# A hybrid decoder layer: the time mixing in three groups of eight heads, two heads' small matmuls side by side

## The chip, the core and the metric

The kernel runs on one core of a Trainium2 chip. The core has a matrix engine (TensorE, PE in the profile), a vector engine (VectorE, DVE), a scalar engine (ScalarE, ACT), a general one (GpSimd, POOL) and a queue that issues DMAs (SyncE, SP). Each works through its own instructions in the order in which they were placed, and waits on semaphores for the others. TensorE writes into eight PSUM banks of 128 partitions x 512 fp32. The metric is the device time of one execution in microseconds.

## What is computed

One layer for 256 tokens of width 4096, in fp32. A normed input is projected once; three mixers use the columns: RWKV-7 time mixing (24 heads of 64 channels), forgetting attention (FoX, 24 heads of 64) and cross attention to 256 memory tokens (4 heads of 256). Their gated outputs go through one output projection, are normed and added to the input.

```python
h = rms_norm(x, g_pre)
p = h @ w_in                                    # 4096 x 14616
# time mixing, for each head, over the tokens t:
Sa = einsum('bhij,bhj->bhi', S, a_t)
S = S * w_t + Sa[..., None] * b_t + v_t[..., None] * k_t
y_t = einsum('bhij,bhj->bhi', S, r_t)
# forgetting attention, for each head:
s = q @ k.T * scale + cum[q] - cum[k]           # causal
o = softmax(s) @ v
# all three:
y = concatenate([y_rwkv * silu(g_rwkv), y_fox * silu(g_fox), y_mem * silu(g_mq)])
out = x + rms_norm(y @ w_out, g_post)
```

## The kernel before

Every weight tile of 512 KB is loaded by SP, split into a high part (ACT, line 193) and a low part (DVE, line 194), and multiplied with the split input. A transposed projection (`proj_t`) of 128 channels does 32 steps of one 512-wide matmul (high part with both parts of the input, line 211) and one 256-wide (low part, line 213) into one accumulator bank of the ring `pj`; `join` (lines 219 to 223) then adds the two halves, ACT reading one and DVE the other. A projection with the tokens on the partitions (`proj_n`, lines 240 to 242) uses two banks and three matmuls a step: the memory values, the FoX values (256 columns at a time) and the output projection (512 columns).

The program has three stages: the memory branch (to about 440 us), the two mixers (to about 1700 us) and the output projection. In the mixers the 24 RWKV heads go in six groups of two pairs. A pair is 128 channels: the even head lies on partitions 0 to 63, the odd one on 64 to 127. `rwkv_group` does, for each pair, the projections of key, receptance and value with the token shift, the decays, the products inside the four chunks of 64 tokens (`gp`, line 529: four chunks of one head, then of the other, 64 x 128 fp32 matmuls, each of two passes) and the transposes of the keys (`bt`, line 539). The gate's projections follow. Then comes the chain: the inverse of a triangular matrix for each head and chunk, in 31 steps of a DVE product and a DVE sum over eight blocks at once (lines 571 and 573) and two sets of 32 x 32 matmuls (`zp`, `ep`, lines 587 and 595); and the four chunks in turn, each with the value transposes (`tv`, line 614), the right-hand side (`rp`, line 619), its copy R (line 621), the update (`up`, line 625), two copies, the state product (`sp`, line 632) and the output (`yp`, lines 642 and 644, pair by pair). Norm, bonus and gate end the group. `fox_pair` does one pair of the forgetting attention: three projections, the logits `sf` (lines 750, 751), softmax, transposes, and the value products `of` (lines 779, 780: one head, then the other). The list FOX_AFTER says which pairs follow which group.

What the small matmuls use of the 128 x 128 array stands in the profile as rows*columns: 64*128 for `gp`, `bt`, `tv` and `sf`, 128*64 for `rp`, `sp`, `of` and the first part of `yp`, 64*64 for `up` and the rest of `yp`, 32*32 for the inverse; the projections use 128*128.

The order on each engine is set by a planner before the run: it takes the program's instructions by priority (the order of the program, with the weight loads and splits ahead) as soon as its own estimate of the times says that their inputs and buffers are there. Where an instruction waits, other ready work is placed ahead of it.

PSUM: three banks for `pj`, two `ch` (chain), two `fx` (FoX), one `el` (the rest of the pairs' work).

Of the kernel before, what the change touches and what calls it, by code (L numbers as in the profile page):

```python
# [8 lines left out]
F32 = mybir.dt.float32  # L9
# [21 lines left out]
# column offsets of the parts of w_in  # L31
# [5 lines left out]
# forgetting-attention pairs that follow each group of the time mixing  # L37
FOX_AFTER = ((0, 1), (2, 3), (4,), (5, 6), (7,), (8, 9, 10, 11))


def _tiles_order():
    t = [("mem", 128 * i) for i in range(8)]
    for h in range(4):
        t += [("in", O_MQ + 256 * h + 128 * j) for j in range(2)]
        t += [("in", O_GM + 256 * h + 128 * j) for j in range(2)]
    t += [("in", O_WL), ("in", O_AL)]
    for g in range(6):
        for o in (O_R, O_K, O_V, O_GR):
            t += [("in", o + 256 * g + 128 * j) for j in range(2)]
        for p in FOX_AFTER[g]:  # L50
            t += [("in", o + 128 * p) for o in (O_FQ, O_FK, O_GF)]
    return t
# [4 lines left out]
# order of the channel tiles of w_out's rows, as they are done (rwkv 0 .. 11, fox 12 .. 23, mem 24 .. 31)  # L57
Y_ORDER = list(range(24, 32)) + list(range(0, 10)) + list(range(12, 22)) + [10, 11, 22, 23]
Y_PLACE = {c: i for i, c in enumerate(Y_ORDER)}

# columns of the constants
C_ID, C_MASK, C_CAUS, C_BLK, C_TRI, C_X0, C_ONE, C_SEL, C_END = 0, 128, 256, 384, 512, 640, 896, 1024, 1048


def _constants():
# [9 lines left out]
    dup = (i % 32) // 8  # L75
    x0 = np.zeros((P, 32, 8), np.float32)
    for d in range(4):
        for k in range(8):
            x0[dup == d, d * 8 + k, k] = 1.0
    c[:, C_X0:C_X0 + 256] = x0.reshape(P, 256)  # L80
# [6 lines left out]
# columns of the per-channel parameters (channel = 128 * column + partition)  # L87
# [10 lines left out]
def pack(inputs):  # L98
# [14 lines left out]
    wV = np.empty((6, P, KT, 256), np.float32)  # L113
    for i in range(6):
        wV[i] = w_in[:, O_FV + 256 * i:O_FV + 256 * i + 256].reshape(KT, P, 256).transpose(1, 0, 2)
    wO = np.empty((8, P, KT, 512), np.float32)
    wo = w_out.reshape(KT, P, D)[Y_ORDER]
    for i in range(8):
        wO[i] = wo[:, :, 512 * i:512 * i + 512].transpose(1, 0, 2)
    wL = np.ascontiguousarray(w_in[:, O_FL:O_FL + NH].reshape(KT, P, NH).transpose(1, 0, 2))  # L120
    # adapters: [128, pair, 128 decay | 128 iclr]
# [11 lines left out]
        "cst": _constants(),  # L133
# [7 lines left out]
class Layer:  # L141
    def __init__(self, tc, a, ctx, dbg=None):
# [9 lines left out]
        self.pj = pool(name="pj", bufs=3, space=PSUM)  # L152
        self.bg = pool(name="bg", bufs=1, space=PSUM)

# [1 line left out]
    def slot(self, name):  # L156
        """two channel tiles, both parts: [128, 2, (high, low), 256]"""
        return self.p4.tile([P, 2, 2, T], F32R, tag="p4", name=name)

    def psb(self, name, tag):  # L160
        return self.bg.tile([P, 512], F32, tag=tag, name=name, bufs=2 if tag != "el" else 1)

    def setup(self):
        nc, cp = self.nc, self.cp
        self.cst = cp.tile([P, C_END], F32, name="cst")
# [9 lines left out]
        ps = self.psb("warm", "fx")  # L175
# [3 lines left out]
        self.blk = self.cst[:, C_BLK:C_BLK + P]  # L179
        self.ones = self.cst[:, C_ONE:C_ONE + P]  # L180
# [16 lines left out]
    def proj_t(self, key, xs, name):  # L197
        """psum [128 columns, 2, 256 tokens] of the weight tile against xs: the sum of both is the product."""
# [17 lines left out]
    def join(self, ps, out, scale=1.0):  # L216
        """scale * (sum of the two halves of a transposed projection)"""
# [7 lines left out]
    def proj_n(self, src, xs, name, pre=None, other=False, late=None):  # L225
        """psum pair [128 tokens, columns]."""
# [19 lines left out]
        for j in range(m):  # L246
# [15 lines left out]
    def rstd_of(self, src, pool, name):  # L262
        """1 / rms of the rows of src: [128 tokens, 2] and as a row on all partitions [128, 256]."""
# [14 lines left out]
        ps = self.psb(f"rb{name}", "el")  # L278
# [6 lines left out]
    def put_y(self, c, y, g, pool):  # L285
        """y * g of channel tile c, kept in DRAM for the output projection."""
# [12 lines left out]
    def mem_phase(self):  # L299
        nc, tc, a = self.nc, self.tc, self.a  # L300
        with tc.tile_pool(name="pm", bufs=2) as pm:
# [3 lines left out]
            def split(i, src, g, ds, rb):  # L305
                """channel tiles 4 i .. 4 i + 3 of src, scaled, into their parts"""
# [18 lines left out]
            for i in range(2):  # L325
# [8 lines left out]
            nc.sync.dma_start(self.cst, a["cst"])  # L334
# [20 lines left out]
            for h in range(4):  # L355
# [9 lines left out]
                sp = self.psb(f"ms{h}", "fx")  # L365
# [16 lines left out]
                tp = self.psb(f"mt{h}", "fx")  # L382
# [6 lines left out]
                op = self.psb(f"mo{h}", "fx")  # L389
# [10 lines left out]
    def shift_mix(self, ps, mu, out, pr, name):  # L400
        """token shift of a [128 channels, 256 tokens] projection."""
# [8 lines left out]
    def head_sums(self, x, name, tag, pr):  # L410
        """sums over the channels of each head, on all of the head's channels."""
        nc = self.nc
        ring = {"tag": "e", "bufs": 8} if tag == "el" else {"tag": "f", "bufs": 3}
        h, l = (pr.tile([P, T], F32R, name=f"{u}{name}", **ring) for u in "hl")
# [7 lines left out]
    def mix_phase(self):  # L422
        nc, tc, a = self.nc, self.tc, self.a
        EV, OD = slice(0, HD), slice(HD, P)
        with tc.tile_pool(name="pr", bufs=1) as pr:
            self.pr = pr
            self.blkr = pr.tile([P, P], F32R, name="blkr")
            nc.vector.tensor_copy(self.blkr, self.blk)
# [433 lines left out]
```

## Time and profile before

| | us |
|---|---|
| median of three executions | 2069.39 |
| lowest, highest | 2068.79, 2069.72 |
| span of the profiled execution | 2068.2 |
| PE busy | 2049.2 (99%) |
| DVE busy | 1358.5 (66%) |
| ACT busy | 1056.1 (51%) |
| weight and other loads | 382.20 MB, 185 GB/s on average |

The busy time of PE is the union of its matmuls, each from its start to a modelled end, and they overlap: a 512-wide matmul lasts 0.40 us in the profile while the next starts 0.23 to 0.24 us later. The share tells whether PE has work, not how fast it does it; what a matmul costs is the distance of the starts in the timeline. A fp32 matmul stands as two instructions in the profile.

### The profile page before, as it was taken

The numbers are of one execution on the slowest core, as the hardware profiler recorded it, in microseconds if no ns is written. First come the engines' busy times: TensorE is split into PE (matmuls) and PEld (weight loads), VectorE is DVE, ScalarE is ACT, GpSimd is POOL, SyncE is SP. The second block draws the span as 40 slices with busy tenths as digits, with TensorE's granted clock in tenths as the row PEclk, the third lists the DMA queues.
The fourth block names the chain that finished last, engine by engine and source line by source line (L and its number), as shares of the span: only waits on it lengthen the run. The fifth ranks groups of instructions, "written<-read, shape, count | busy, mean of one in ns | idle before, by whom it ended". The sixth has DMA issues, their size and how long they took to land.

```text
span 2068.2 us, 31727 instructions
## 1 busy us (share of the span) xinstructions
PE 2049.2 (99%) x12352; PEld 1735.4 (84%) x12352; DVE 1358.5 (66%) x2108; ACT 1056.1 (51%) x1529; POOL 116.3 (6%) x220
## 2 busy tenths in 40 slices
PE   9999999999999999999999999999999999999997
PEld 7888888888988898889888888888898887888886
DVE  6565444476866786678868847797795566444445
ACT  7644544455456544645555455545545456444443
POOL 0292000000000000000000000000000001000000
PEclk9999999999999999999999999999999999999999
DMA  9865555555544555455535544554454468666665
GB/s 364 314 220 180 175 180 171 182 188 173 176 162 144 171 179 166 148 172 167 174 133 167 176 155 141 183 171 154 137 186 147 152 211 287 213 199 198 199 198 183
DMA packets 111274, 382.20 MB, mean 185 GB/s; under 512 B 12540, under 2 KB 17812, under 8 KB 111124
## 3 DMA queue, kind: packets, MB, share of 16 engines
q1 hardware_dynamic: 109332, 373.88, 54.4%
q0 software_dynamic: 1792, 6.29, 0.9%
q8 instruction: 97, 1.59, 0.3%
q14 instruction: 53, 0.43, 0.1%
HBM read 372.23 MB, written 7.89 MB: 184 GB/s over the span
## 4 chain that ended last, share of the span: by engine, by line
PE 96%; POOL 1%; DVE 1%; ACT 1%; DMA 1%; issue 0%; SPq 0%; DVEq 0%; ACTq 0%; POOLq 0%
PE pno L241 5%; PE pno L242 5%; PE pno L240 5%; PE pjkr L211 4%; PE pjq6400f L211 4%; PE pjvr L211 4%; PE pjrr L211 4%; PE pjq7936f L211 4%; PE pjgr L211 4%; PE pjgf L211 4%; PE pjmq L211 3%; PE pjgm L211 3%; PE pnfv L240 2%; PE pnfv L242 2%; PE pnfv L241 2%; PE pjkr L213 2%
## 5 line engine op out<-in xcount | busy, mean ns | idle before, releaser
L194 DVE TENSOR_TENSOR wlno<-rawno,whno 128x1024 fp32r<-128x1024 f32 x128 | 156.6, 1225 | 160.8 <-ACT whno L193 160.7
L193 ACT ACTIVATE whno<-rawno 128x1024 fp32r<-128x1024 f32 x128 | 135.4, 1060 | 173.6 <-PE pno L242 158.2
L241 PE MATMUL pno<-wlno,yp 128*128 128x512 f32 x512 | 199.7, 390 | 1.1 <-DVE wlno L194 1.1
L242 PE MATMUL pno<-whno,yp 128*128 128x512 f32 x512 | 199.3, 389 | 0.0
L240 PE MATMUL pno<-whno,yp 128*128 128x512 f32 x512 | 180.5, 390 | 0.6 <-ACT whno L193 0.6
L211 PE MATMUL pjvr<-x,whvr 128*128 128x512 f32 x384 | 139.9, 401 | 0.0
L211 PE MATMUL pjkr<-x,whkr 128*128 128x512 f32 x384 | 139.1, 400 | 0.0
L211 PE MATMUL pjrr<-x,whrr 128*128 128x512 f32 x384 | 138.9, 399 | 0.0
L211 PE MATMUL pjq6400f<-x,whq6400f 128*128 128x512 f32 x384 | 138.6, 400 | 0.0
L211 PE MATMUL pjgf<-x,whgf 128*128 128x512 f32 x384 | 137.6, 399 | 0.0
L211 PE MATMUL pjq7936f<-x,whq7936f 128*128 128x512 f32 x384 | 136.9, 397 | 0.0
L211 PE MATMUL pjgr<-x,whgr 128*128 128x512 f32 x384 | 135.1, 395 | 0.0
L241 PEld LDWEIGHTS pno<-wlno,yp 128*128 128x128 f32 x512 | 96.1, 188 | 22.0 <-DVE wlno L194 2.2
L240 PEld LDWEIGHTS pno<-whno,yp 128*128 128x128 f32 x512 | 96.0, 188 | 21.4 <-ACT whno L193 1.4
L242 PEld LDWEIGHTS pno<-whno,yp 128*128 128x128 f32 x512 | 96.1, 188 | 20.1
L242 PE MATMUL pnfv<-whnfv,x 128*128 128x256 f32 x384 | 109.5, 286 | 0.0
L241 PE MATMUL pnfv<-wlnfv,x 128*128 128x256 f32 x384 | 109.2, 285 | 0.0
L240 PE MATMUL pnfv<-whnfv,x 128*128 128x256 f32 x384 | 109.1, 287 | 0.0
L213 PE MATMUL pjkr<-x,wlkr 128*128 128x256 f32 x372 | 106.2, 285 | 0.0
L213 PE MATMUL pjvr<-x,wlvr 128*128 128x256 f32 x372 | 106.1, 285 | 0.0
L213 PE MATMUL pjrr<-x,wlrr 128*128 128x256 f32 x372 | 105.8, 284 | 0.0
L213 PE MATMUL pjgf<-x,wlgf 128*128 128x256 f32 x372 | 105.5, 284 | 0.0
(422 smaller groups left out, 5461.6 us busy)
## 6 DMA issues: line engine op xcount, KB each, us to landing
rawno<-in_wO SPq DMA_DIRECT2D x128, 512.0 KB, 4.4
rawkr<-in_wT SPq DMA_DIRECT2D x48, 512.0 KB, 3.5
rawrr<-in_wT SPq DMA_DIRECT2D x48, 512.0 KB, 3.5
rawvr<-in_wT SPq DMA_DIRECT2D x48, 512.0 KB, 3.6
rawgr<-in_wT SPq DMA_DIRECT2D x48, 512.0 KB, 3.6
rawnfv<-in_wV SPq DMA_DIRECT2D x48, 512.0 KB, 3.5
rawq6400f<-in_wT SPq DMA_DIRECT2D x48, 512.0 KB, 3.7
rawq7936f<-in_wT SPq DMA_DIRECT2D x48, 512.0 KB, 3.7
```

The source lines that it names most:

```text
L193: nc.scalar.activation(wh, raw, AF.Copy)
L194: nc.vector.tensor_tensor(wl, raw, f32(wh), ALU.subtract)
L211: nc.tensor.matmul(ps, wh[:, k, :], x.rearrange("p u t -> p (u t)"), start=(kt == 0), stop=last)
L213: nc.tensor.matmul(ps[:, 0:T], wl[:, k, :], x[:, 0, :], start=False, stop=False)
L240: nc.tensor.matmul(ps[t], xh, w[0][:, k, :], start=(kt == 0), stop=False)
L241: nc.tensor.matmul(ps[t], xh, w[1][:, k, :], start=False, stop=False)
L242: nc.tensor.matmul(ps[t], xl, w[0][:, k, :], start=False, stop=(kt == KT - 1))
```

## The change

The RWKV heads go in three groups of four pairs, eight heads (GP = 4), and the code of a group is split in parts: `group_tiles`, `rwkv_pair`, `rwkv_chain`, `rwkv_norm`. A FoX group of four pairs follows each; its values are projected 512 columns at a time (`fox_values`), and the gate's projection and the norm of a pair come after the FoX pairs. The products inside the chunks, the transposes and the FoX logits and value products alternate between the two heads of a pair, which write to two PSUM banks (the value products: to two halves of one). The transposes of the values of all chunks stand in the pair's part beside those of the keys. In the chain the matmuls of all eight heads follow one another in each step, the first half of the output behind the right-hand side, the second behind the state product. `after` makes the first matmul of such a run wait for the last of the run's inputs. The inverse does 16 blocks at once; its start matrix comes by a DMA, and the group's tiles have one buffer instead of two. `proj_n` does the weight tile's steps for the first half of the tokens and then for the second. PSUM: two banks `pj`, three `sm`, two `ch`, one `yp`. The rows of `w_out` are packed in the new order.

```diff
-        self.pj = pool(name="pj", bufs=3, space=PSUM)
+        self.pj = pool(name="pj", bufs=2, space=PSUM)
...
-        return self.bg.tile([P, 512], F32, tag=tag, name=name, bufs=2 if tag != "el" else 1)
+        return self.bg.tile([P, 512], F32, tag=tag, name=name, bufs={"sm": 3, "ch": 2, "yp": 1}[tag])
+
+    def after(self, ins, *others):
+
+        for o in others:
+            self.tc.add_manual_dep(ins.ins, o.ins.name, mybir.DependencyInfo(
+                mybir.DependencyClass.Sync, mybir.DependencyReason.DATA), reason="together")
...
-            for k in range(kc):
-                for t in range(2):
+            for t in range(2):
+                for k in range(kc):
                     mul(j, k, t, w)
...
-                for g in range(6):
-                    self.rwkv_group(g, lr, pr)
-                    for kp in FOX_AFTER[g]:
-                        self.fox_pair(kp, pf)
+                for g in range(NG_):
+                    G = self.group_tiles(g, pr)
+                    for p in range(GP):
+                        self.rwkv_pair(g, p, G, lr, pr)
+                    self.rwkv_chain(g, G, pr)
+                    self.fox_values(g, pf)
+                    for i, norms in enumerate(((0, 1), (2,), (3,), ())):
+                        self.fox_pair(GP * g + i, pf)
+                        for p in norms:
+                            self.rwkv_norm(g, p, G, pr)
...
+        sl = (slice(1, 3), slice(0, 2))
+        gp = [self.psb(f"gp{n}{u}", "sm").rearrange("p (c k t) -> p c k t", c=NCH, k=2) for u in range(2)]
+        for c in range(NCH):
+            for u, hf in enumerate(half):
+                m = nc.tensor.matmul(gp[u][:, c], BK[hf, c, sl[u], :], Tt[u][hf, p, c], start=True, stop=True)
+                if c == u == 0:
+                    self.after(m, at)
...
+        tp = [self.psb(f"bt{n}{u}", "sm").rearrange("p (k c j) -> p k c j", k=2, c=NCH) for u in range(2)]
+        for c in range(NCH):
+            for u, hf in enumerate(half):
+                o = CH * (c + u)
+                nc.tensor.transpose(tp[u][:, 1, c], vp[hf, o:o + P], self.ident[hf, hf])
+        for c in range(NCH):
+            for u, hf in enumerate(half):
+                nc.tensor.transpose(tp[u][:, 0, c], BK[hf, c, sl[u], :], self.ident[hf, hf])
+        for u, hf in enumerate(half):
+            of = half[1 - u]
+            nc.scalar.activation(BKn[:, :, p, u, :], tp[u][:, 0], AF.Copy)
+            nc.scalar.activation(SU[of, :, p, u, :], tp[u][of, 1], AF.Copy)
...
+        X = pr.tile([P, 32, U], F32, name=f"X{N}", tag="X")
+        nc.sync.dma_start(X, a["x0"])
...
+        for c in range(NCH):
+            heads = [(p, u, hf) for p in range(GP) for u, hf in enumerate(half)]
+            rp, yp = ps("rp", c), ps("yp", c, "yp")
+            for p, u, hf in heads:
+                m = nc.tensor.matmul(rp[hf, p, :], Tt[u][:, p, c, 0, :], SU[:, c, p, u, :], start=True, stop=True)
+                if ready is not None and p == u == 0:
+                    self.after(m, ready)
+            for p, u, hf in heads:
+                nc.tensor.matmul(yp[hf, p, :], SU[:, c, p, u, :], Tt[u][:, p, c, 1, :], start=(p == 0), stop=False,
+                                 skip_group_check=True)
+            R = RR[:, c % 2]
+            nc.vector.tensor_copy(R, rp)
+            up = ps("up", c)
+            for p, u, hf in heads:
+                nc.tensor.matmul(up[hf, p, :], Et[hf, NCH * p + c, :], R[hf, p, :], start=True, stop=True)
+            nc.vector.tensor_copy(SU[EV, c, :, 0, :], up[EV])
+            ready = nc.scalar.activation(SU[OD, c, :, 1, :], up[OD], AF.Copy)
+            if c < NCH - 1:
+                sp = ps("sp", c)
+                for p, u, hf in heads:
+                    m = nc.tensor.matmul(sp[hf, p, :], BKn[:, c, p, u, :], SU[:, c, p, u, :], start=True, stop=True)
+                    if p == u == 0:
+                        self.after(m, ready)
+            for p, u, hf in heads:
+                m = nc.tensor.matmul(yp[hf, p, :], SU[hf, c, p, u, :], NG[hf, p, c, 1, :], start=False,
+                                     stop=(p == GP - 1), skip_group_check=True)
...
+    def fox_values(self, g, pf):
+
+        self.vn = pf.tile([P, 2, 512], F32, tag="vn", name=f"vn{g}")
+        ps = self.proj_n(self.a["wV"][g], self.xs, f"fv{g}")
+        for t in range(2):
+            self.nc.scalar.activation(self.vn[:, t, :], ps[t], AF.Copy)
...
+        op = self.psb(f"o{n}", "sm")[:, 0:T]
+        for t in range(2):
+            for u, hf in enumerate(half):
+                c = 128 * (kp % GP) + HD * u
+                m = nc.tensor.matmul(op[hf, P * t:T], vn[:, t, c:c + HD], pts[u][:, T * t:T + P * t],
+                                     start=(t == 0), stop=(t == 1))
+                if t == u == 0:
+                    self.after(m, ready)
```

## Rows read from the trace of the kernel before

**Rows 1.** The page: busy time of each engine, its share of the span, instructions
```profile
PE 2049.2 (99%) x12352; PEld 1735.4 (84%) x12352; DVE 1358.5 (66%) x2108; ACT 1056.1 (51%) x1529; POOL 116.3 (6%) x220
```

**Rows 2.** Waits of PE: waiting group, whom for, us in all, times, longest
```profile
PE pjmk L213 <- DVE wlmk L194: 2.4, 3, 0.9
```

**Rows 3.** Busy time, mixers' stretch: PE, PEld, DVE, ACT, POOL, clock, DMA share
```profile
440.00:1700.00 1260.00, 1260.00 (x8463) 1073.22 (x8462) 928.44 (x1603) 660.27 (x995) 21.76 (x115) 1.00 0.50 164
```

**Rows 4.** Timeline of PE around one run: start, length (us), line, tiles, shapes
```profile
465.78 0.28 PE L213 MATMUL pjrr<-x,wlrr 128*128 128x256 f32 x1
465.90 0.40 PE L211 MATMUL pjrr<-x,whrr 128*128 128x512 f32 x1
466.14 0.28 PE L213 MATMUL pjrr<-x,wlrr 128*128 128x256 f32 x1
466.35 1.16 PE L529 MATMUL gpr<-T0r,BKr 64*128 64x128 f32 x8
467.44 0.51 PE L211 MATMUL pjrr<-x,whrr 128*128 128x512 f32 x1
467.78 0.28 PE L213 MATMUL pjrr<-x,wlrr 128*128 128x256 f32 x1
```

**Rows 5.** Timeline of PE, transposes: keys, values of one head, of both
```profile
479.33 0.46 PE L539 MATMUL btr<-cst,BKr 64*128 64x64 f32 x4
...
608.22 0.33 PE L614 MATMUL tvr<-cst,vpr 64*128 64x64 f32 x2
...
628.86 0.34 PE L614 MATMUL tvr<-cst,vpr 64*128 64x64 f32 x4
```

**Rows 6.** Timeline of PE: chunk steps, with the matmul that follows the long run
```profile
603.91 0.45 PE L632 MATMUL spr<-SUr,BKnr 128*64 128x64 f32 x8
...
605.20 0.50 PE L211 MATMUL pjgf<-x,whgf 128*128 128x512 f32 x1
...
622.69 0.33 PE L632 MATMUL spr<-SUr,BKnr 128*64 128x64 f32 x2
...
637.13 0.45 PE L625 MATMUL upr<-Rr,Etr 64*64 64x64 f32 x8
```

**Rows 7.** Timeline of PE: attention logits of a pair, value products of a head
```profile
574.75 0.50 PE L750 MATMUL sf<-q7936f,q6400f 64*128 64x128 f32 x4
575.07 0.61 PE L751 MATMUL sf<-q7936f,q6400f 64*128 64x256 f32 x4
...
635.27 0.65 PE L779 MATMUL of<-ptf,vn 128*64 128x256 f32 x2
635.75 0.38 PE L780 MATMUL of<-ptf,vn 128*64 128x128 f32 x2
```

**Rows 8.** Busy time of one tile's instructions: pnfv (256 wide), pno (512 wide)
```profile
1157.00:1166.00 9.00, 9.00 (x78) 9.00 (x77) 0.00 (x0) 1.00 0.48 157
...
1900.00:1950.00 50.00, 50.00 (x222) 41.43 (x221) 1.38 (x2) 1.35 (x4) 1.00 0.63 201
```

**Rows 9.** Groups of DVE by line: count, busy us, mean ns, idle before
```profile
L571 DVE TENSOR_TENSOR tmr<-NNr,Xr 128x16 f32<-128x16 f32 (+30 forms) x186 | 79.7, 429 | 4.3
...
L573 DVE TENSOR_REDUCE Xr<-tmr 128x8 f32<-128x16 f32 (+30 forms) x186 | 54.1, 291 | 3.9
```

**Rows 10.** Timeline of DVE: the copy ahead of the update
```profile
633.32 0.29 DVE L621 COPY Rr<-rpr 128x128 f32<-128x128 f32 x1
```

**Rows 11.** Timeline: last matmul of a projection (PE), last read of its bank (DVE)
```profile
574.42 0.39 PE L211 MATMUL pjgf<-x,whgf 128*128 128x512 f32 x1
...
579.72 0.42 DVE L221 TENSOR_TENSOR gf<-pjgf,gf 128x256 f32<-128x256 f32 x1
```

**Rows 12.** Timeline: one chain's first inverse step, block product, last output copy
```profile
530.94 2.02 DVE L564 STREAM_TRANSPOSE NNr<-NGr 128x1024 f32<-128x1024 f32 x1
...
578.99 0.69 PE L587 MATMUL zpr<-Enr,NGr 32*32 32x32 f32 x32
...
664.65 0.28 ACT L645 ACTIVATE Yr<-ypr 128x128 f32<-128x128 f32 x1
```

More of the change, by code (lines that the diff above doesn't have):

```diff
@@ L46, in _tiles_order @@
     t += [("in", O_WL), ("in", O_AL)]
-    for g in range(6):
[L48 to L51, printed above, removed]
+    for g in range(NG_):
+        for p in range(GP * g, GP * g + GP):
+            t += [("in", o + 128 * p) for o in (O_K, O_R, O_V)]
+        for p in range(GP * g, GP * g + GP):
+            t += [("in", o + 128 * p) for o in (O_FQ, O_FK, O_GF, O_GR)]
     return t
@@ L84, in _constants, with _x0 @@
     return c
+def _x0():
+    dup = (np.arange(P) % 32) // 16
+    x0 = np.zeros((P, 32, 16), np.float32)
+    for d in range(2):
+        for k in range(16):
+            x0[dup == d, d * 16 + k, k] = 1.0
+    return x0
 _PCOLS = [("g_pre", 32), ("g_mem", 32), ("mu_rwkv", 38), ("w0", 12), ("a0", 12), ("k_k", 12),
@@ L112, in pack @@
         wN[i] = w_mem[:, 1024 + 512 * i:1536 + 512 * i].reshape(KT, P, 512).transpose(1, 0, 2)
-    wV = np.empty((6, P, KT, 256), np.float32)
-    for i in range(6):
-        wV[i] = w_in[:, O_FV + 256 * i:O_FV + 256 * i + 256].reshape(KT, P, 256).transpose(1, 0, 2)
+    wV = np.empty((3, P, KT, 512), np.float32)
+    for i in range(3):
+        wV[i] = w_in[:, O_FV + 512 * i:O_FV + 512 * i + 512].reshape(KT, P, 512).transpose(1, 0, 2)
     wO = np.empty((8, P, KT, 512), np.float32)
@@ L553, in rwkv_group @@
-        for p in range(2):
-            gps = self.proj_t(("in", O_GR + 128 * (2 * g + p)), self.xs, f"g{N}{p}")
-            self.join(gps, gt[:, p, :])
-            nc.scalar.activation(gt[:, p, :], gt[:, p, :], AF.Silu)
+        Tt, NG, PC, BKn, SU = (G[k] for k in ("T", "NG", "PC", "BKn", "SU"))
+        U = GP * NCH
         ng = NG.rearrange("p a c k t -> p (a c) k t")
@@ L582, in rwkv_group @@
                 nc.gpsimd.memset(Et[rows, :, 0:32], 0.0)
[L584 to L585 removed]
+        zp = self.psb(f"zp{N}", "ch").rearrange("p (u c) -> p u c", u=U)
+        for u in range(U):
             for o in (0, 64):
@@ L588, in rwkv_group @@
                                  start=True, stop=True)
-        Z = f("Z", (P, 8, 32))
-        for o in (32, 96):
-            nc.scalar.activation(Z[o:o + 32], zp[o:o + 32], AF.Copy)
-        ep = self.psb(f"ep{N}", "ch")[:, 0:256].rearrange("p (u c) -> p u c", u=8)
-        for u in range(8):
-            for o in (0, 64):
-                nc.tensor.matmul(ep[o:o + 32, u, :], Z[o + 32:o + 64, u, :], Et[o + 32:o + 64, u, 32:64],
-                                 start=True, stop=True)
-        for o in (0, 64):
-            nc.scalar.activation(Et[o:o + 32, :, 32:64], ep[o:o + 32], AF.Copy)
@@ new lines, in rwkv_chain @@
+        for u in range(U):
+            for o in (0, 64):
+                m = nc.tensor.matmul(ep[o:o + 32, u, :], Z[o + 32:o + 64, u, :], Et[o + 32:o + 64, u, 32:64],
+                                     start=True, stop=True)
+                if u == o == 0:
+                    self.after(m, last)
+        nc.scalar.activation(Et[0:32, :, 32:64], ep[0:32], AF.Copy)
+        nc.vector.tensor_copy(Et[64:96, :, 32:64], ep[64:96])
+        G["Y"] = Y = pr.tile([P, GP, T], F32, name=f"Y{N}", tag="NN")
@@ L616, in rwkv_group @@
-            rp = self.psb(f"rp{N}{c}", "ch")[:, 0:P].rearrange("p (a i) -> p a i", a=2)
-            for p in range(2):
-                for u, hf in enumerate(half):
-                    nc.tensor.matmul(rp[hf, p, :], Tt[u][:, p, c, 0, :], SU[:, p, u, 0, :], start=True, stop=True)
-            R = pr.tile([P, 2, HD], F32, name=f"R{N}{c}", tag="R", bufs=2)
-            nc.vector.tensor_copy(R, rp)
-            up = self.psb(f"up{N}{c}", "ch")[:, 0:P].rearrange("p (a i) -> p a i", a=2)
-            for p in range(2):
-                for u, hf in enumerate(half):
-                    nc.tensor.matmul(up[hf, p, :], Et[hf, 4 * p + c, :], R[hf, p, :], start=True, stop=True)
@@ L639, in rwkv_group @@
-            yp = self.psb(f"yp{N}{c}", "ch")[:, 0:P].rearrange("p (a t) -> p a t", a=2)
-            for p in range(2):
-                for u, hf in enumerate(half):
-                    nc.tensor.matmul(yp[hf, p, :], SU[:, p, u, 0, :], Tt[u][:, p, c, 1, :], start=True, stop=False)
-                for u, hf in enumerate(half):
-                    nc.tensor.matmul(yp[hf, p, :], SU[hf, p, u, 1, :], NG[hf, p, c, 1, :], start=False, stop=True)
-            nc.scalar.activation(Y[:, :, CH * c:CH * c + CH], yp, AF.Copy)
```

389 lines of the change are left out of this document (184 added, 205 removed).

## The prediction

> **What bounds the kernel now.** I read the page first: PE is busy 99% of the span, DVE 66%, ACT 51% [rows 1]. A busy PE can still be waiting, so the next view is PE's own waits: the longest group is 2.4 us in all, in the memory branch [rows 2]; no PE wait at all stands against a small matmul. Then the stretch of the two mixers, 440 to 1700 us, where nearly the whole change lies: PE is busy for all of it at a granted clock of 1.00, the 2.4 GHz level, while DVE is at 928 of 1260 us and DMA at half [rows 3]. So the time is what TensorE's queue takes from start to start, and an edit is worth what it takes out of that queue, unless it makes PE wait. "Busy" does not show that cost (matmuls overlap); the starts in the timeline do.
>
> **What a run of small matmuls costs.** In [rows 4] the big projection matmuls start 0.12 us (256 wide) and 0.24 us (512 wide) after one another. The 256-wide one ahead of the eight score products (L529, on 64 rows of the array) keeps the queue 0.21 us instead, and the 512-wide one behind them 0.34 us. From 466.14 to 467.78 is 1.64 us; less 0.12 and 0.24 the run costs 1.28, which is 0.12 more than its row's own length of 1.16. I price every run that way: length plus 0.12. Two lengths separate the work from the fee for going to another tiling of the array and back: four key transposes of one head take 0.46 and two value transposes 0.33, so a transpose is 0.065 us, and 0.46 + 0.12 - 4 x 0.065 = 0.32 us is the fee of a run [rows 5].
>
> **Two heads at once.** Four value transposes, two of each head (rows 0 to 63 and 64 to 127, each head's result in a bank of its own), take 0.34 us where two of one head take 0.33 [rows 5]. The second head is nearly free. The planner did that by chance here; in the score products it does not occur, since one head's four chunks are written ahead of the other's.
>
> **The change, part by part** (cost on PE's queue, before and after).
>
> Score products: 24 runs x 1.28 = 30.7 us. After: 12 runs with both heads interleaved. If the second head is free, each is as long as one head's run: 12 x 1.28 = 15.4, a gain of 15. If it is not, only 12 fees go: 4. I take 15, as [rows 5] is the same use of 64 rows and two banks.
>
> Transposes: keys 24 x (0.46 + 0.12) = 13.9 us. Values, 48 sets of two: 19 stand alone (0.45 each), 16 lie in eight runs of four (0.46 a run) and 13 join another run (some 0.25), together 15.5. After: the values move out of the chunk steps into the pair's stage, each with both heads interleaved. The keys are ready before the values are mixed, so I count two runs a pair, each 0.58: 13.9. Gain 15.5; 9 if the heads don't overlap (24 x 0.26 more), 19 if both sets go as one run. The copies out of PSUM move along (ACT, half as many and twice as long); no DMA goes with them.
>
> Chunk steps, 24 of them: recurrence right-hand side (like L625), update, and the state/output run: 0.57 + 0.57 + 1.48 = 2.62 us [rows 6] (the last from 603.91 to 605.20, plus 0.19 as 1.28 - 1.09 in [rows 4]). 24 x 2.62, less 6 x 0.23 as the last chunk has no state product, is 61.5; in about 24 places a piece breaks off, as the two at 622.69, at 0.33 + 0.12 each: 72. After: 12 steps of eight heads. Eight matmuls in 0.57 - 0.32 make 0.06 us a pair of heads. A step is 16 pairs (right-hand side and the first half of the output) 1.28, 8 pairs (update) 0.80, and 16 pairs with one change of tiling inside 1.43 (0.15: what 1.48 leaves over 12 pairs and 0.32, in three); 3.51, and 2.88 in the last chunk. 3 x (3 x 3.51 + 2.88) = 40, plus 2 for pieces. Gain 30, bounded by 20 (pieces at the same rate as now) and 32.
>
> Inverse: its two block products fall from 12 runs to 6; 6 x 0.32 = 2.
>
> FoX: the logits already run with both heads interleaved in most pairs [rows 7], so 0. The value products: 0.65 at 635.27 with 0.38 from 635.75 is 0.86, with 0.12 0.98 a head; x24 = 23.5, less 2 as 11 stand right behind another run. After, 12 runs for both heads side by side in columns: 12 if the heads overlap, 12 x (2 x 0.98 - 0.32) = 19.7 if not. The 64-wide ones overlap in columns (0.06 a pair above), a 256-wide pair alone is not shown. I take 12: gain 9.5, bound 2.
>
> FoX values: 1152 matmuls of 256 columns become 576 of 512. 78 in 9.28 us (the last one's 0.28 hangs over) is 0.119 each, 222 in 50.4 is 0.227 [rows 8]: 137 against 131, gain 6. The Trainium skill (TensorEngine Tiling, Instruction Overhead) gives each matmul some 60 cycles; at 2.4 GHz the 576 that go would be worth 14 us, an estimate from that page, and the time 8 us less than forecast. The row shows 2 x 0.119 - 0.227 = 0.011 us for each that goes, under half of it, and the row decides.
>
> Runs of the new kernel will also stand behind one another now and then; at today's rate that is 2 more. Sum of gains: 15 + 15.5 + 30 + 2 + 9.5 + 6 + 2 = 80.
>
> **What lies on other engines.** The inverse's 31 steps run for 16 blocks at once in 3 groups: 93 pairs of operations instead of 186, each at most twice as long, so at most today's 79.7 + 54.1 us of DVE [rows 9]. DVE stays below 80% of the shorter stretch. The matrix X comes by a 256 KB DMA on SP, not a POOL copy: SP's queue holds the weight loads, so a wait for X's buffer would stop those; the buffer's last user is the group before, over 100 us earlier, so 0. Gate projections and norms move behind the chain and only change places with other PE work. Two waits are new. First, the explicit one ahead of each run: all of PE's queue stands behind it. Its cover today: the copy of R ends at 633.61 and the update starts at 637.13, 3.5 us later [rows 6, 10]; so 0; if that cover went, 36 runs would each wait out the rest of a copy, a microsecond or two, some 50 us. Second, projection accumulators fall from three to two banks. A wide FoX-values product needs both free. A projection's last read today ends 5.3 us after its last matmul (574.42 + 0.39 to 579.72 + 0.42) [rows 11]; 1.4 us of six matmuls run before the second bank is needed, so at three places PE stands 0 to 4 us: 0 to 12, and I take 6.
>
> Net 80 - 6 = 74. The profiled span is 2068.2 us, the median 1.2 above it: 2068.2 - 74 + 1.2 = 1995 us.
>
> **Rivals.** (1) The change doesn't do all it says: the planner, which places each instruction by its own estimates, breaks the runs up, or two heads overlap less when each product is two passes of fp32. Then the gains are 4, 9, 20 and 2 in the four places: 35 us less, 2030. For it: about 24 broken steps today; against: [rows 5].
> (2) The chain outlasts its cover, since the group's tiles have one buffer now and the next group can't write them. Today a chain takes from 530.94 to 664.65, 134 us [rows 12], 48 of it inverse. With a doubled inverse it is 182. The cover is a values product (192 x 0.227 = 44) and 16 projections of 32 x 0.36 us: 228. If the chunk steps grew by half as well (86 to 129 us), it would be 225, just inside; 20 us beyond in each group would put the time at 2055.
> (3) Slower: the accumulators. With two banks a projection stands still once the join of the one before last takes over 11.5 us; each of the 84 projections in the mixers would have to lose 0.95 us to eat 80, so joins of 12.5 us where the row has 5.3 (during an inverse, when DVE is fullest). The price at 13 us of join: 84 x 1.5 = 126, less 80: 2115. The Trainium skill (TensorEngine Tiling, PSUM Bottleneck) warns of this: tiling quickens TensorE and not the copies out of PSUM, which can become the bottleneck. The row leaves a factor of two.
>
> **How the numbers follow.** Forecast 0.80, (1) 0.10, (2) 0.05, (3) 0.05. The range's low end takes the better bounds: transposes 3.5, pieces 2, no stall at the banks 6, and 8 for wider merging of runs: 1975. The high end is rival (1) with the stall at 12: 2036. Beyond it lie (2), (3) and a tail: 0.15. About 0.2% (4 us) is what a measurement of this kernel tells from no change. Faster: all but (3) and the far end of (2): 0.93; same 0.02; slower 0.05.
>
> **What would show it.** Right: PE still at 99% with no wait on a small matmul; runs of 16 score products of some 1.16 us; 24 transpose runs near 0.46; three runs a chunk step; values products at 0.227. Wrong: score runs near 2 us; PE waits on the accumulators (idle ahead of L240 or L211) or at the runs' first matmuls; a stretch before the second and third group where PE waits on the chain; a clock below 1.00.

## The result and the profile after

The changed kernel takes 2009.03 us (median of four executions, 2008.06 to 2009.81) beside 2069.09 us of the kernel before on the same chip: a ratio of 0.9708, with a 95% interval of 0.9695 to 0.9722. That is 60 us off, where 74 were forecast. The profiled execution has a span of 2008.0 us. Line numbers from here on are those of the changed kernel.

The page's line of busy times (as in [rows 1]):

```profile
PE 1985.8 (99%) x11776; PEld 1677.8 (84%) x11776; DVE 1317.5 (66%) x1856; ACT 1033.6 (51%) x1439; POOL 113.1 (6%) x196
```

The mixers' stretch (columns as in [rows 3]). The window is put 60 us shorter; in the traces it is 1221.0 us from the first receptance, key or value projection of the mixers to the first matmul of the output projection, where it was 1284.3:

```profile
440.00:1640.00 1200.00, 1198.82 (x7909) 1017.67 (x7908) 889.59 (x1356) 640.58 (x910) 18.28 (x97) 1.00 0.57 173
```

PE's waits (as in [rows 2]):

```profile
PE pno L254 <- DVE wlno L207: 2.8, 3, 1.7
PE pjmk L226 <- DVE wlmk L207: 2.5, 3, 0.9
...
PE tf L823 <- DVE Lf L820: 1.0, 4, 0.4
PE pnfv L254 <- DVE wlnfv L207: 0.7, 3, 0.2
...
PE pjmq L224 <- DVE mk L234: 0.4, 1, 0.4
```

So nothing changed in what bounds the kernel: PE has work for the whole stretch at a granted clock of 1.00, DVE is at 890 of 1200 us, and none of the waits listed stands before a matmul on another tiling than 128*128. Most wait for a part of a weight tile (`wl`, the low part, in three of these). New, beside the short ones at the FoX values (`pnfv`), are two: the FoX transposes `tf` wait for DVE's part of the softmax, and in the memory branch a projection, `pjmq`, waits for DVE's last read of an accumulator bank (the join of `mk`, line 234).

The timeline of PE, which answers [rows 4 to 7]:

```profile
468.70 0.28 PE L226 MATMUL pjrr<-x,wlrr 128*128 128x256 f32 x1
468.91 0.37 PE L552 MATMUL gpr<-T0r,BKr 64*128 64x128 f32 x1
468.92 0.37 PE L552 MATMUL gpr<-T1r,BKr 64*128 64x128 f32 x1
469.13 0.27 PE L552 MATMUL gpr<-T0r,BKr 64*128 64x128 f32 x1
...
469.80 0.27 PE L552 MATMUL gpr<-T1r,BKr 64*128 64x128 f32 x1
469.91 0.40 PE L572 MATMUL btr<-cst,vpr 64*128 64x64 f32 x4
470.15 0.41 PE L575 MATMUL btr<-cst,BKr 64*128 64x64 f32 x4
470.49 0.50 PE L224 MATMUL pjrr<-x,whrr 128*128 128x512 f32 x1
...
474.74 0.46 PE L572 MATMUL btr<-cst,vpr 64*128 64x64 f32 x4
475.04 0.41 PE L575 MATMUL btr<-cst,BKr 64*128 64x64 f32 x4
...
524.78 0.33 PE L656 MATMUL ypr<-T0r,SUr 128*64 128x64 f32 x2
525.04 0.38 PE L226 MATMUL pjvr<-x,wlvr 128*128 128x256 f32 x1
...
669.29 0.33 PE L672 MATMUL ypr<-NGr,SUr 64*64 64x64 f32 x2
669.54 0.50 PE L224 MATMUL pjgr<-x,whgr 128*128 128x512 f32 x1
669.98 0.69 PE L668 MATMUL spr<-SUr,BKnr 128*64 128x64 f32 x16
670.59 0.68 PE L672 MATMUL ypr<-NGr,SUr 64*64 64x64 f32 x14
...
680.72 0.68 PE L662 MATMUL upr<-Rr,Etr 64*64 64x64 f32 x16
681.34 0.39 PE L226 MATMUL pjgr<-x,wlgr 128*128 128x256 f32 x1
...
737.94 0.87 PE L831 MATMUL of<-ptf,vn 128*64 128x256 f32 x8
738.74 0.50 PE L224 MATMUL pjgr<-x,whgr 128*128 128x512 f32 x1
```

Three things are to be seen. The score products go as forecast: T0 and T1 start together, sixteen instructions in 1.00 us (468.91 to 469.91), where eight of one head took 1.09 with the change of tiling behind them [rows 4]. The transposes come one head at a time: four and four of the first head directly behind the products (no fee of their own), those of the second head almost 5 us later in a run of their own. And pieces of the output, two instructions each (one matmul), stand by themselves, at 524.78 in the middle of the pairs' stage and at 669.29 just ahead of the run to which they belong.

Where the 60 us come from. I went through PE's matmuls behind the memory branch in the order of their starts and called every stretch on another tiling than 128*128 a run; its price is the time that it puts between the 128*128 matmuls around it, beyond their usual 0.12 and 0.23 us. The kernel before has 199 runs with 511 changes of tiling, 180.2 us in all; the changed one 108 with 243, 118.4 us: 61.8 off. The FoX values fell from 138.2 to 132.6: 5.6 off. Some 7 came back: the mixers start 2.2 later (at 420.3 us, where it was 418.1), the output projection has 1.7, gate and value projections 2 to 3, the rest below 1 each.

### The profile page after: what moved, and what is told of

It reads as the page before. It is cut to its first block, busy times and chain, and to the rows that moved or that the text cites. A ratio compares the mean times of both kernels' runs of the same rounds, so it can differ in the third digit from the quotient of the medians.

```text
span 2008.0 us, 30242 instructions
## 1 busy us (share of the span) xinstructions
PE 1985.8 (99%) x11776; PEld 1677.8 (84%) x11776; DVE 1317.5 (66%) x1856; ACT 1033.6 (51%) x1439; POOL 113.1 (6%) x196
## 4 chain that ended last, share of the span: by engine, by line
PE 94%; DVE 2%; POOL 2%; DMA 1%; ACT 1%; issue 1%; DVEq 0%; SPq 0%; ACTq 0%; POOLq 0%
PE pno L254 6%; PE pno L255 6%; PE pno L253 6%; PE pjq7936f L224 5%; PE pjkr L224 5%; PE pjq6400f L224 4%; PE pjrr L224 4%; PE pjvr L224 4%; PE pjgr L224 4%; PE pjgf L224 4%; PE pjmq L224 3%; PE pjgm L224 3%; PE pjq6400f L226 2%; PE pjvr L226 2%; PE pjgr L226 2%; PE pjq7936f L226 2%
## 5 line engine op out<-in xcount | busy, mean ns | idle before, releaser
L253 PE MATMUL pno<-whno,yp 128*128 128x512 f32 x512 | 180.2, 390 | 0.0
L226 PE MATMUL pjgr<-x,wlgr 128*128 128x256 f32 x372 | 106.6, 286 | 0.0
L226 PE MATMUL pjq6400f<-x,wlq6400f 128*128 128x256 f32 x372 | 105.6, 284 | 0.0
L226 PE MATMUL pjq7936f<-x,wlq7936f 128*128 128x256 f32 x372 | 104.8, 282 | 0.0
```

Of the source, the lines that this page charges most:

```text
L226: nc.tensor.matmul(ps[:, 0:T], wl[:, k, :], x[:, 0, :], start=False, stop=False)
L253: nc.tensor.matmul(ps[t], xh, w[0][:, k, :], start=(kt == 0), stop=False)
```

## The experiments

Every kernel ran beside the kernel before on one chip, whose median there was 2069.1 to 2071.3 us. Across chips I therefore compare ratios: 0.0010 is 2.1 us, and two ratios closer than about 0.0020 (4 us) are not told apart by these intervals alone.

**1. The broken-off pieces.** The forecast of 42 us for the chunk steps measures 54.5. The difference is 24 pieces of the output, two or four instructions (one or two matmuls) each, that stand alone: 18 x 0.46 + 6 x 0.47 = 11.1 us, nearly all of it fees. Their inputs are ready early: in chunk 0 the state is zero, so the first half of the output needs only a pair's T; and the first head's second half needs only DVE's copy of the update, not ACT's, for which the state product waits. The edit gives both the wait of their run:

```diff
-        nc.vector.tensor_copy(Et[64:96, :, 32:64], ep[64:96])
+        first = nc.vector.tensor_copy(Et[64:96, :, 32:64], ep[64:96])
...
+                m = nc.tensor.matmul(yp[hf, p, :], SU[:, c, p, u, :], Tt[u][:, p, c, 1, :], start=(p == 0), stop=False,
...
+                if c == 0:
+                    self.after(m, first)
...
                 m = nc.tensor.matmul(yp[hf, p, :], SU[hf, c, p, u, :], NG[hf, p, c, 1, :], start=False,
...
+                if p == u == 0:
+                    self.after(m, ready)
```

> The changed kernel (2009 us) with two more explicit waits: the first half of the output of chunk 0 waits for the end of the inverse, and the second half of every output for the last copy of the update, so that no output matmul runs ahead of its run. Theory 'pieces': the chunk steps gained less than forecast because 24 runs of one to four matmuls break off the output, at 0.46 us each = 11.1 us; whole, they add some 1.5 us to the runs they belong to: 2009 - 9.6 = 1999 us, with no run of two output matmuls left in the timeline. Rival 'steps': the runs of a chunk step themselves cost more than I summed (3.51 us), and the pieces are harmless as PE always has work: within 2 us of 2009.

Measured: 1999.21 us, ratio 0.9659 (0.9644 to 0.9673), 10 us faster than the changed kernel. PE's timeline has the run whole:

```profile
666.54 0.39 PE L224 MATMUL pjgr<-x,whgr 128*128 128x512 f32 x1
666.86 0.68 PE L670 MATMUL spr<-SUr,BKnr 128*64 128x64 f32 x16
667.47 0.68 PE L674 MATMUL ypr<-NGr,SUr 64*64 64x64 f32 x16
668.09 0.38 PE L226 MATMUL pjgr<-x,wlgr 128*128 128x256 f32 x1
```

87 runs are left, at 105.8 us in all, 12.6 less. The pieces are the cause; the steps themselves cost what was forecast (54.5 - 12.6 is 42).

**2. The transposes' banks.** The second head's transposes wait for a bank: the score products hold two of the three `sm` banks, and DVE's last read of the first of these ends at 471.78 us, after the first head's transposes are done:

```profile
471.09 0.69 DVE L559 TENSOR_TENSOR T0r<-gpr,cst 64x512 f32<-64x512 f32 x1
```

The edit puts the transposes into the two `ch` banks, which are idle in the pairs' stage, and lets them wait for the mixed values (`vl`, the last operation of the values' token shift):

```diff
-        tp = [self.psb(f"bt{n}{u}", "sm").rearrange("p (k c j) -> p k c j", k=2, c=NCH) for u in range(2)]
+        tp = [self.psb(f"bt{n}{u}", "ch").rearrange("p (k c j) -> p k c j", k=2, c=NCH) for u in range(2)]
...
-                nc.tensor.transpose(tp[u][:, 0, c], BK[hf, c, sl[u], :], self.ident[hf, hf])
+                m = nc.tensor.transpose(tp[u][:, 0, c], BK[hf, c, sl[u], :], self.ident[hf, hf])
+                self.after(m, vl)
```

> The changed kernel with the transposes of keys and values in the chain's two PSUM banks (in place of the three shared ones), all of them waiting for the mixed values. Theory 'banks': the two heads' transposes come one head after the other in the changed kernel because the score products hold two of the three shared banks; with two free banks they interleave and stand as one run behind the score products: from 1.78 + 0.83 = 2.61 us a pair to 1.28 + 8 x 0.063 = 1.78, times 12 = 10 us less, 1999 us. If they stand together but the heads do not overlap: 12 fees of 0.33 alone, 2005 us. Rival 'order': the planner, not the banks, sets them apart, or the longer run waits for the values: 2009 us or more.

Measured: 2002.91 us (2000.89 to 2005.44), ratio 0.9678 (0.9663 to 0.9692), 6 us faster; the profiled execution, the fastest of the four, took 2000.89. So the time lies between the first two cases, and the timeline decides for overlap:

```profile
469.65 0.41 PE L572 MATMUL btr<-cst,vpr 64*128 64x64 f32 x8
469.89 0.42 PE L575 MATMUL btr<-cst,BKr 64*128 64x64 f32 x8
470.24 0.39 PE L435 MATMUL bsr<-hbsr,blkr 128*128 128x256 f32 x1
```

Eight transposes of two heads take the 0.41 us that four of one head took at 470.15, and the twelve runs of a second head are gone: 110.8 us of runs, 7.6 less. Part of what was missing to the 10 us of the first case is a wait that grew from 1.0 to 2.9 us:

```profile
PE tf L824 <- DVE Lf L821: 2.9, 3, 1.0
```

Both heads' transposes can run at once. That it was the banks which kept them apart in the changed kernel rests on this run and the DVE row above; the edit moves the banks and adds a wait, and no run separates the two.

**3. Heads in turn or one after the other.** Score products and FoX value products written head after head, all else as in the changed kernel:

```diff
-        for c in range(NCH):
-            for u, hf in enumerate(half):
+        for u, hf in enumerate(half):
+            for c in range(NCH):
                 m = nc.tensor.matmul(gp[u][:, c], BK[hf, c, sl[u], :], Tt[u][hf, p, c], start=True, stop=True)
...
```

> The changed kernel with the score products and the FoX value products written one head after the other again, in the same runs. Theory 'overlap': the second head is nearly free when interleaved, so in turn the score products take 12 x 8 x 0.112 = 10.7 us more and the value products 12 x 0.64 = 7.7 us more: 2009 + 18 = 2027 us. Rival 'fees': the gain comes from fewer runs alone, which stay the same in number: 2009 us.

Measured: 2011.78 us, ratio 0.9717 (0.9700 to 0.9733), 2 us slower, which the intervals don't tell from no change: near the case that I had called fees only, but not for its reason. PE's timeline:

```profile
469.63 0.82 PE L552 MATMUL gpr<-T0r,BKr 64*128 64x128 f32 x5
470.18 0.37 PE L552 MATMUL gpr<-T1r,BKr 64*128 64x128 f32 x1
470.29 0.27 PE L552 MATMUL gpr<-T0r,BKr 64*128 64x128 f32 x1
470.39 0.27 PE L552 MATMUL gpr<-T1r,BKr 64*128 64x128 f32 x1
...
470.74 0.28 PE L572 MATMUL btr<-cst,vpr 64*128 64x64 f32 x1
470.84 0.27 PE L552 MATMUL gpr<-T1r,BKr 64*128 64x128 f32 x1
470.85 0.28 PE L572 MATMUL btr<-cst,vpr 64*128 64x64 f32 x2
```

In PE's queue all eight instructions of T0 stand before those of T1, yet T1's first starts beside T0's fifth, and T1's last ones run beside the first head's transposes: 1.94 us a run instead of 1.78. The nine runs of FoX value products by themselves cost 9.0 us in either order. (The number of runs did not stay the same: six more pieces of the output broke off, 114 runs.) The Trainium skill (TensorE: Matmul & The Clock Gate, Part 3: Packing small matmuls, The mechanism) says that matmuls start and end strictly in the order of the program; here, in all 12 pairs, the first instruction on the other half of the rows starts ahead of three that stand before it, and the measurement decides. So overlap does not need the heads to alternate. A second run, on the best kernel (5, below), tested that with numbers: products and transposes both head after head.

> The kernel labelled best with the score products and the transposes of a pair written head after head (eight instructions of one head, eight of the other) instead of in turn. It follows the run labelled turn, where the score products in that order cost 2 us in all and not 18: its timeline shows the second head's first product starting beside the fifth of the first head. Theory (an instruction for one half of the rows can start while up to four of the other half still stand ahead of it): of a pair's 32 small matmuls the first four stand alone, then four and four overlap at each change of head, the last four alone: 12 x 0.112 + 8 x 0.063 = 1.85 instead of 8 x 0.112 + 8 x 0.063 = 1.40 us, +0.45 for each of 12 pairs, 5 us: 1993. Rival (no such look-ahead; turn was saved by something else, such as the transposes behind): each head by itself, 16 x 0.112 + 16 x 0.063 = 2.80, +1.40 a pair, 17 us: 2004. Rival (the order does not matter at all): 1987.

Measured: 1993.89 us, ratio 0.9628 (0.9613 to 0.9642), 6.6 us slower than the best kernel; a pair's run takes 2.33 us instead of 1.78, so 0.55 more where 0.45 was expected. The look-ahead stands as a description of these traces; what makes it was not tested.

**4. The second head in a run of its own.** On the best kernel, the second head's products wait for the first head's masked ones:

```diff
...
         for u, hf in enumerate(half):
             of = half[1 - u]
+            for c in range(NCH):
+                m = nc.tensor.matmul(gp[u][:, c], BK[hf, c, sl[u], :], Tt[u][hf, p, c], start=True, stop=True)
+                if c == 0:
+                    self.after(m, at)
             nc.vector.tensor_tensor(NG[hf, p], gp[u][hf], mb(hf), ALU.mult)
-            nc.vector.tensor_tensor(Tt[u][of, p], gp[u][of], mb(of), ALU.mult)
+            at = nc.vector.tensor_tensor(Tt[u][of, p], gp[u][of], mb(of), ALU.mult)
```

> The kernel labelled best, with the second head's score products made to wait for the masked products of the first head, so that they make a run of their own, as in the kernel before; the planner then also puts most transposes into a run of their own (90 runs in place of 69). It undoes the pairing of the heads in the score products. Theory (a run pays its fee of 0.32 to 0.38 us, and the second head is free only within one run): 21 runs of eight products at 1.28, 9 runs of transposes at 0.88 and 3 of both at 1.78 make 40.1 us instead of 12 x 1.78 = 21.4: 19 more, 2006. Rival (what counts is the number of runs only, the second head's work is not free): 21 x 0.35 = 7 more, 1995.

Measured: 2017.61 us, ratio 0.9741 (0.9727 to 0.9756), 30 us slower. PE's timeline shows a head's products back at the length of [rows 4]:

```profile
469.82 1.16 PE L554 MATMUL gpr<-T0r,BKr 64*128 64x128 f32 x8
470.90 0.51 PE L224 MATMUL pjrr<-x,whrr 128*128 128x512 f32 x1
471.34 0.46 PE L571 MATMUL btr<-cst,vpr 64*128 64x64 f32 x8
```

The runs' total rose from 95.1 to 114.6 us, 19.5 where 18.7 was worked out: in the runs, pairing is worth what the prices say. The other 9 us of the span were not expected. Of these, 5.7 are waits at the head sums of a norm, once in each group, which the planner now put where their inputs are not there:

```profile
PE vvr L435 <- ACT hvvr L432: 5.7, 3, 1.9
```

**5. Best kernel, and the size of the groups.** Best is edits 1 and 2, and the first update of chunk 0 waits for the end of the inverse too.

```diff
...
+                m = nc.tensor.matmul(up[hf, p, :], Et[hf, NCH * p + c, :], R[hf, p, :], start=True, stop=True)
+                if c == p == u == 0:
+                    self.after(m, first)
```

> The changed kernel with both edits of before at once (the output's pieces tied to their runs; the transposes in the two chain banks, waiting for the mixed values), and the first update of chunk 0 of each group waits for the end of the inverse as well. Theory (the time is what the tensor engine's queue is kept by runs of small matmuls, and these gains add): the first edit took 9.9 us off, the second 6.1 by its median, and three broken-off updates are some 2 more: 1991, between 1988 and 1994. Rival (the two edits remove partly the same fees, since the pieces stood in the stage of the transposes): 1997 or more. Rival (the waits begin to cost: with all small work in whole runs the tensor engine stands before them): above 1999, with waits shown ahead of the runs' first matmuls.

Measured: 1987.34 us (1986.95 to 1988.10), ratio 0.9596 (0.9582 to 0.9609). 69 runs, 95.1 us: 23.3 less than the changed kernel, of which edits 1 and 2 had taken 12.6 and 7.6. The gains add, and the median is 4 us below the estimate, which had been built on the second edit's median and not on its profile. Then the same with GP = 2, six groups of four heads (inverse of eight blocks, two buffers for the group's tiles):

> The kernel labelled best, with six groups of four heads instead of three of eight; FoX values stay 512 wide (every second group), the group's tiles have two buffers. This isolates the size of the groups. Theory (a step of four heads pays the same fees for half the work): a chunk step of eight heads measures 1.28 + 0.81 + 1.42 = 3.51 us, one of four 0.80 + 0.56 + 0.95 = 2.31, so 24 x 2.31 - 12 x 3.51 = 13.3, and six block products of the inverse more at 0.32 make 15: some 2006. Rival (what grouping brought was mostly that fewer pieces break off, which best has removed otherwise): 1996 or less. Rival (smaller groups leave the chain more cover): no slower than best.

Measured on the same chip: 2014.49 us, ratio 0.9728 (0.9714 to 0.9741), 27 slower than the best kernel, where 15 had been worked out. The runs' total is 113.9 us, 18.8 more: the 15, and the rest because some pieces break off again. Of the other 8, 5.7 are waits near the end, at the norms of the last group, which has fewer FoX projections behind it than a large one; the longest groups of them:

```profile
PE vvr L435 <- ACT hvvr L432: 3.1, 2, 1.7
...
PE mpr L436 <- DVE lmpr L433: 1.2, 1, 1.2
...
PE mpr L435 <- ACT hmpr L432: 0.9, 1, 0.9
```

**6. The added waits.** The changed kernel with `after` emptied:

```diff
-        for o in others:
...
+        return
```

> The changed kernel without the added waits ahead of each run's first matmul (each matmul then waits for its own inputs only, as in the kernel before). Theory (the waits cost nothing where they stand, since their cover is long, and keep the runs whole): 120 runs in place of 108, 12 x 0.35 = 4 us slower, 2013. Rival (the waits hold the tensor engine up, as half a microsecond to two at 36 runs would): faster than 2009 by several us. Rival (the planner's order makes the runs by itself): 2009.

Measured: 2013.92 us, ratio 0.9731 (0.9715 to 0.9747), 4.8 slower than the changed kernel by the ratios. 120 runs, 124.9 us: 6.5 more. So the waits keep the runs whole, and the changed kernel's trace shows no idle time of PE ahead of a run's first matmul (the best kernel's does, three times 0.14 us).

**7. The width of the FoX values.** Two products of 256 columns a group in the changed kernel:

> The changed kernel with the FoX values projected 256 columns at a time, in two products a group, one after the other. Theory (by the rows, 2 x 0.119 - 0.227 = 0.011 us for each of 576 matmuls): 5.6 to 6 us slower than the changed kernel, 2015. The rule of the Trainium skill (TensorEngine Tiling, Instruction Overhead: some 60 cycles a matmul) would make it 14 us, 2023. Rival (three more products want two accumulators each, as in the forecast's term of 2 us a place): 6 us more on top of the 6, 2021, with idle time of the tensor engine ahead of the second product's first matmuls.

Measured: 2014.64 us, ratio 0.9727 (0.9714 to 0.9741), 4 to 6 us slower (3.9 by the ratios, which alone would not tell it from no change, 6.2 by the spans); in its trace the values take 138.8 us against 132.6. The row's 0.011 us a matmul holds. The 14 us that the rule of the Trainium skill (TensorEngine Tiling, Instruction Overhead: some 60 cycles a matmul) would make, read as a cost that each matmul adds, are not there. The section goes on to say that a matmul of one column takes as long as one of 60; read so, as the least that a short matmul takes, it says nothing against the row.

**8. Two accumulators.** Three runs. The kernel before with two `pj` banks instead of three:

> The kernel before (2069 us) with two projection accumulators instead of three, nothing else: the cost that I put at 6 us (0 to 12) for three hand-overs, here at six FoX values products. Theory after the result (three stalls of 0.4 us stand in the trace of the changed kernel): at most 6 x 0.5 = 3 us more, 2069 to 2072 us. The forecast's price: 6 x 2 = 12 us more, 2081 us. Rival 3 of the forecast (joins outlast a projection): 2080 us and above, with PE waits ahead of the projections all through the mixers.

Measured: 2079.17 us, ratio 1.0046 (1.0031 to 1.0061), some 9.5 slower, more than I had come to think after seeing the result and near the forecast's price. The longest of PE's waits name weights; in the memory branch two projections wait for a bank, `pjmk` (for a copy, 0.8 us) and `pjmq`:

```profile
PE pno L240 <- ACT whno L193: 2.5, 1, 2.5
PE pnfv L241 <- DVE wlnfv L194: 1.6, 2, 1.1
...
PE pjmq L211 <- DVE mk L221: 0.7, 1, 0.7
```

The FoX values cost 3.3 us more there and the output projection 3.3, the runs 1.7 (201 of them), and the mixers start 0.8 later: 9.1 of the 10.6 between the spans. The second run puts the old order of matmuls (both halves of the tokens in turn) back into the changed kernel:

> The changed kernel with the old order of matmuls in a product that has the tokens on the partitions: a weight tile's steps go through both halves of the tokens in turn, so that the second accumulator is wanted after three matmuls and not after six. Theory (the new order is what keeps the hand-over of two accumulators cheap: the changed kernel shows about 0.4 us of idle time at each FoX values product and some 3.7 at the output projection's starts): 0.7 us more at each of three values products and up to 5 at the output projection's, 2012 to 2016. Rival (the order makes no difference, the banks are free by then): 2009. Rival (alternating halves is better, since each half's weights arrive sooner): faster than 2008.

Measured: 2009.70 us, ratio 0.9703 (0.9690 to 0.9716): no difference. The third gives the best kernel its third accumulator back, at the cost of one `sm` bank:

> The kernel labelled best with three accumulator banks for the projections again, and two instead of three for the small matmuls. It tests the forecast's term for the hand-over of two accumulators (6 us, at the three FoX values products). Theory (two accumulators hold nothing up in the new kernel: the idle time at the values products, 0.4 us each, is a wait for the low part of a weight tile): nothing is gained, and the lost bank breaks nine runs off (78 in place of 69), some 3 us: 1990. Rival (the forecast's term is right): 6 us faster, less those 3: 1984, and the idle time at the values products gone.

Measured: 1988.36 us, ratio 0.9606 (0.9590 to 0.9622): not told apart from the best kernel. 78 runs cost 4.7 us more, and in the profiled executions, which both have a span of 1985.7 us, about as much comes back: 1.7 before the mixers start, 1.6 at the output projection, 1.1 at the values. In the memory branch it is the bank: `pjmq` waits for the join of `mk` in every kernel here with two accumulators (0.9 us in the best one) and in neither with three. The stall of 0.4 us at each values product is gone, but one of 0.7 has come at a gate's projection, again for a low part:

```profile
652.26 0.40 PE L224 MATMUL pjgr<-x,whgr 128*128 128x512 f32 x1
653.23 0.39 PE L226 MATMUL pjgr<-x,wlgr 128*128 128x256 f32 x1 [0.58 <-DVE wlgr L207]
```

So by these two traces two accumulators cost some 4 us in the best kernel too, and the bank that they leave for the small matmuls is worth as much. Why weight parts come late at the values and the output projection when there are two accumulators stays open.

## Why the prediction was right, and where it was not

The time fell inside the range, 14 us above the forecast, and for the reason given: PE's queue, counted in fees and overlaps. Point by point:

- *The price of a run* held: 108 runs were taken apart with length plus 0.12, and edits that merged or split runs moved the time by the prices so found (runs 1, 4 and 6).
- *Score products*, 15: 12 runs of 16 at 1.28 us (sixteen products alone, before the transposes that stand behind them) against 24; 15 measured.
- *Transposes*, 15.5: 16.0 us are left (12 x 0.50 and 12 x 0.83) instead of 13.9, gain 13.4. The total was near, the step was not: I had two runs a pair with both heads overlapped, and it became one head behind the products and one alone. The step that failed is that both heads' banks are free at once; run 2, in which they are, has 7.6 us less in its runs.
- *Chunk steps*, 30: the term that was mis-sized. It measured 72 - 54.5 = 17.5, below the bound of 20. Within a step all is as worked out (3.5 us; update 0.81, right-hand side and output 1.28 to 1.32, state and output 1.42 when whole). I had put 2 us for pieces, by the rate of today; there are 24 of them, because the changed code holds back only the first matmul of a run, and these are ready earlier and have no wait of their own. Rival (1) named this mechanism, with 35 us in four places, 10 of them here; it took 12.
- *Inverse*: DVE's groups of [rows 9] are now

```profile
L606 DVE TENSOR_TENSOR tmr<-NNr,Xr 128x32 f32<-128x32 f32 (+30 forms) x93 | 59.9, 644 | 2.2
L608 DVE TENSOR_REDUCE Xr<-tmr 128x16 f32<-128x32 f32 (+30 forms) x93 | 40.6, 437 | 2.1
```

  100.5 us of DVE, where today's 133.8 were the bound (half as many at 1.5 times the length); PE's block products as forecast.
- *FoX value products*, 9.5: eight in 1.00 us (the run at 737.94 with its fee), 9.0 us for nine runs and some 3 for the three that stand beside an update: 12, as taken. A pair of 256 columns starts 0.01 apart, so they overlap in columns as the 64-wide ones do.
- *FoX values*, 6: 5.6 (run 7).
- *Accumulators*, -6: the sum lost some 7 us to idle time and longer spacing. The size was near, the place was not: the term had PE stand at the values products until a bank is free, and what is lost there is 1.1 us (three stalls of 0.4) for the low part of a weight. The wait for a bank is in the memory branch, 0.4 us. By the traces a third accumulator gave back some 4 us in three places (experiment 8); that the 7 are the accumulators' cost is not shown.
- *Rival (2)*, the chain: from the inverse's first transpose (DVE's timeline) to the last output copy (ACT's) it takes 135 us, as before [rows 12], where 182 were feared:

```profile
587.55 2.04 DVE L599 STREAM_TRANSPOSE NNr<-NGr 128x1024 f32<-128x1024 f32 x1
```

```profile
722.54 0.38 ACT L684 ACTIVATE Yr<-ypr 128x256 f32<-128x256 f32 x1 [0.29 <-PE ypr L672]
```

- *Rival (3)*, joins that eat the gain: the one PE wait on an accumulator among those listed is the 0.4 us in the memory branch; in the mixers there is none, also with 256-wide copies in the chunks.

Sum: 15.3 + 13.4 + 17.5 + 9.5 + 2 from the terms, 4 that the terms don't place (runs that stand behind one another, for which 2 were counted), 5.6 from the values, less 7: 60.

## What to carry to other kernels

Where the matrix engine is never idle, count its changes of tiling and not its busy time: here a run of small matmuls costs 0.3 to 0.4 us beyond its work, and a wait on its first matmul keeps only that one back, so every matmul of the run that is ready earlier needs the same wait. Before counting on two heads side by side, see which PSUM banks are free at that moment; the order in which the two are written matters less than that they stand in one run.

## What was not expected of the hardware

A small matmul for one half of the array's rows started while three earlier instructions for the other half had not (470.18 us in the fence of run 3); two heads written one after the other cost 0.17 us a pair more than in turn, where 0.9 would be no overlap (8 x 0.112). The Trainium skill (TensorEngine Tiling, Key Properties) says that a change of tiling mode drains the engine; the traces agree that it costs, and give the price: 69 runs with 162 changes and 199 with 511 differ by 85 us, in which overlap has a part, and a piece of one 64-wide matmul (two instructions, 0.33 us long) alone keeps the queue 0.46.
